# Normed residuals handed on by halves of the tokens, 1/rms taken under further projections, and linear attention values written twice with zero rows

## The chip, the cores and the metric

The kernel runs on one core of a Trainium2 chip. The metric is the device time of one execution in microseconds (us). The engines of the core are TensorE (PE, with its weight loads listed as PEld), VectorE (DVE), ScalarE (ACT), GpSimd (POOL) and SyncE (SP), which here issues the DMAs.

## The reference, cut to what matters

Two transformer blocks in sequence on one sequence of 512 tokens with 1024 features, all in fp32. The first is a hybrid layer whose mixer and feed-forward outputs are normed before they are added; the second has an even and an odd layer, with plain residuals.

```python
# first block (hybrid_layer)
mix = jnp.concatenate([o_a, o_s], axis=-1) @ w_out
x = x + rms_norm(mix, post_mix_norm)
h = rms_norm(x, pre_ffn_norm)
u = causal_dwconv(h @ w_up, ffn_conv_w, ffn_conv_b)
gate, up = jnp.split(u, 2, axis=-1)
f = (jax.nn.silu(gate) * up) @ w_down
x = x + rms_norm(f, post_ffn_norm)
# second block, for layer 0 (even) and 1 (odd)
x = x + mixer(rms_norm_2(x, mix_norm))
x = x + conv_ffn(rms_norm_2(x, ffn_norm[layer]), ...)
# odd mixer: gated linear attention over 8 chunks of 64 tokens, 4 heads, dk 128, dv 256
def step(state, inp):
    q_c, k_c, v_c, decay_c = inp
    state = decay_c[..., None] * state + jnp.einsum('bchk,bchv->bhkv', k_c, v_c)
    return state, jnp.einsum('bchk,bhkv->bchv', q_c, state)
```

## The kernel before, in words

The residual X is kept as 8 tiles of 128 features (partitions) x 512 tokens. The program is a sequence of stages: mix1, ffn1 (the first block), even, ffn2, odd, ffn3 (the second). Every stage projects with weights that come by DMA. A projection is done in split precision: the weight is cast into a hi part by ACT (`wload`, L197) and its rest, the lo part, by DVE (L200), the activations likewise, and `mm3` (L209 to L211) issues three matmuls for each block of 128 features: hi x hi, hi x lo, lo x hi, each 128 x 128 weights against 512 tokens. Of a 1024 x 128 weight tile, the 8 blocks make 24 matmuls, here called one projection.

A norm before a projection isn't applied to the activations: the projection takes X times the gain, and the result is scaled by 1/rms of each token afterwards. So a stage's first projections need only the hi and lo parts of X times the gain (`prep_block`: hi by ACT L261, lo by DVE L262, the square by ACT L287, the sum of squares in `acc` by POOL or, for the last, DVE L289). `first` (L297) runs the first four projections of the next stage block by block as these come; inside, `stat_r` (L323) takes column sums of `acc` by PE (st, L328) and makes 1/rms, and `bcast` (L334) spreads it over the partitions by a ones matmul (bc, L341).

mix1 and ffn1 end in `post_norm`: the output projection's blocks m = 0 to 7 are the generator `gen`; each block is squared (ACT L430) and summed (POOL L435); after block 7 two ones matmuls for each half of the tokens (pb, L441 and L443) give the sum over features; ACT makes 1/rms (L445 to L447), DVE corrects it (L449, L450), and then for each of the 8 blocks DVE forms F times gain times r (L457; L451 for block 0) and adds it to X (L458; L452), and `emit` prepares the next stage's activations. The first of these can start only when all of block 7 is done.

In the odd mixer, each head has 8 chunks of 64 tokens. The values V are written from PSUM by ACT (L1128), two blocks of 128 tokens in one tile. For each chunk the matmul pS (L1218) contracts the 64 tokens, that is 64 partitions, of the decayed keys KD and of V, DVE updates the state S (L1224), and two matmuls po (L1227) apply it to the chunk's queries. While this chain runs, the projection of the next head's values (or, for the last head, the output projection) is put between.

The order on each engine is made by a scheduler that goes through the program with priorities, each instruction going where its inputs and buffers allow; the chain of the odd mixer is put at a higher priority (HP). PSUM tiles for projections come from the pools pp and pm; weight tiles have 4 buffers for hi and 4 for lo, raw weights 2, activations 32 ("act").

Of the kernel before, what the change touches and what calls it, by code (L numbers as in the profile page):

```python
# [90 lines left out]
class Prog:  # L91
# [98 lines left out]
    def wload(s, src, f):  # L190
# [4 lines left out]
        hi = s.sb.tile([P, 1024], F32R, tag="wh", bufs=NBUF["wh"], name=s.nm("wh"))  # L195
        lo = s.sb.tile([P, 1024], F32R, tag="wl", bufs=NBUF["wl"], name=s.nm("wl"))
# [31 lines left out]
    def proj_part(s, src, per, n, acts):  # L228

        for i in range(KB // per):  # L230
            hi, lo = s.wload(src[i], per * n * P)
            for j in range(per):
# [4 lines left out]
                yield i * per + j, out  # L237

# [53 lines left out]

    def take(s):

        return s.acts, s.R, s.rb

    def first(s, srcs, late=True):  # L297
# [23 lines left out]
        s.ready += outs  # L321

# [42 lines left out]
    def ffn(s, wu, wd, cw, cb, norm=False):  # L365
# [40 lines left out]
    def add_res(s, X, gen, nxt):  # L406
        for m, ps in gen:
            if m == 0:
                s.begin(nxt)
            s.nc.vector.tensor_add(X[m], X[m], ps)  # L410
            s.emit(m, X[m])
        s.finish(False)

    def post_norm(s, gen, gain, X, nxt, part=None):
# [4 lines left out]
        F = []  # L419
        ng = s.small(KB, tag="ng", bufs=1)  # L420
        v.tensor_scalar(ng, s.pv[:, PVO[gain]:PVO[gain] + KB], -1.0, None, ALU.mult)
        for m, ps in gen:
            sq = s.t(tag="u") if m else acc
            if part is None:
                f, fs = s.act(F32), ps
            else:
                f = fs = part[m]
                v.tensor_add(f, f, ps)
            for h in ([slice(0, S // 2), slice(S // 2, S)] if m == KB - 1 else [slice(0, S)]):
                sc.activation(sq[:, h], fs[:, h], AF.Square)  # L430
            if part is None:
                sc.copy(f, ps)
            F.append(f)
            if 0 < m < KB - 1:
                nc.gpsimd.tensor_tensor(acc, acc, sq, ALU.add)  # L435

        pbs = [s.pt("pb"), s.pt("pb")]
        r = s.sb.tile([P, S], F32, tag="rb", bufs=2, name=s.nm("rb"))
        halves = [slice(0, S // 2), slice(S // 2, S)]
        for pb, h in zip(pbs, halves):  # L440
# [974 lines left out]
```

## Time and profile before

| What | Value |
|---|---|
| median of 3 runs (lowest to highest) | 2184.18 us (2183.92 to 2188.77) |
| the profiled execution: its time, its span | 2189.66 us, 2187.9 us |
| granted clock, mean over the span | 0.98 |
| PE busy | 2106.9 us, 96% |
| DVE, ACT, POOL busy | 65%, 43%, 9% |

The span is from the first to the last instruction of the profiled execution; times in rows are microseconds from the span's start. PE's matmuls are pipelined, so a row's duration is longer than the distance from one start to the next; costs are read from starts. The granted clock is a share of full speed: 1.00 is 2.4 GHz and 0.50 is 1.2 GHz.

### The profile page before, as it was taken

To read this page: it belongs to the slowest core of one execution; us is meant where nothing else is said; L and a number is where in the kernel's file an instruction comes from. 1 tells how busy PE (TensorE), PEld (TensorE's weight loads), DVE (VectorE), ACT (ScalarE), POOL (GpSimd) and SP (SyncE) were. 2 spreads that over 40 slices of the span, in tenths; PEclk is the share of its full clock that TensorE was granted. 3 is DMA by queue.
4 is the path that set the end of the run, shared out by engine and by line. 5 is a ranking of instruction groups with operands and counts; after the bars stand their busy time and mean duration, and the time that the engine had idled before them with its cause. 6 is when DMAs were issued, how large, how long until landed. Compare 5 with 4: busy or idle time off the path is not lost.

```text
span 2187.9 us, 26672 instructions
## 1 busy us (share of the span) xinstructions
PE 2106.9 (96%) x10260; PEld 1734.5 (79%) x10260; DVE 1418.1 (65%) x2540; ACT 933.2 (43%) x1506; POOL 198.2 (9%) x137
## 2 busy tenths in 40 slices
PE   7999899989989999998999999999999999999999
PEld 6777788777768888886877788888889877888887
DVE  6788867787568777226887787763343566877621
ACT  5444453355435444224665444442242324444411
POOL 3211111133030000012000100000000001000000
PEclk9999999999989999999999999999999999999999
DMA  4222212132213222321211132223322112322332
GB/s 151 97 64 84 78 64 74 68 104 99 87 39 126 97 96 93 94 93 48 96 46 61 58 124 97 97 91 98 93 71 95 55 61 68 118 99 99 93 114 66
DMA packets 57526, 189.14 MB, mean 86 GB/s; under 512 B 7757, under 2 KB 8013, under 8 KB 57398
## 3 DMA queue, kind: packets, MB, share of 16 engines
q1 hardware_dynamic: 55042, 180.75, 25.1%
q0 software_dynamic: 2032, 6.59, 0.9%
q8 instruction: 81, 1.33, 0.2%
q14 instruction: 47, 0.39, 0.1%
q10 hardware_dynamic: 324, 0.09, 0.0%
HBM read 184.99 MB, written 2.41 MB: 86 GB/s over the span
## 4 chain that ended last, share of the span: by engine, by line
PE 82%; DVE 13%; ACT 2%; DMA 1%; issue 1%; POOL 0%; SPq 0%; DVEq 0%; ACTq 0%; POOLq 0%
PE pp L209 24%; PE pp L211 23%; PE pp L210 23%; DVE wl L200 1%; DVE a L262 1%; DVE xbc L361 1%; DVE qkv L361 1%; DVE s L654 1%; PE pS L1218 1%; PE pz L979 1%; PE po L1227 1%; PE py L854 1%; DVE s L655 1%; PE pU L680 1%; DMA a<-bdd 1%
## 5 line engine op out<-in xcount | busy, mean ns | idle before, releaser
L209 PE MATMUL pp<-a,wh 128*128 128x512 f32 x2048 | 817.3, 400 | 15.6 <-ACT a L261 10.5
L210 PE MATMUL pp<-a,wh 128*128 128x512 f32 x2048 | 812.0, 397 | 1.3 <-DVE a L270 0.9
L211 PE MATMUL pp<-a,wl 128*128 128x512 f32 x2048 | 811.9, 397 | 0.9 <-DVE wl L200 0.9
L197 ACT CAST wh<-wr 128x1024 fp32r<-128x1024 f32 (+2 forms) x331 | 340.0, 1028 | 552.6 <-PE pp L210 420.6
L200 DVE TENSOR_TENSOR wl<-wr,wh 128x1024 fp32r<-128x1024 f32 (+3 forms) x300 | 362.2, 1207 | 230.4 <-ACT wh L197 223.0
L209 PEld LDWEIGHTS pp<-a,wh 128*128 128x128 f32 x2048 | 389.5, 190 | 102.7 <-ACT a L261 11.3
L210 PEld LDWEIGHTS pp<-a,wh 128*128 128x128 f32 x2048 | 389.3, 190 | 84.6 <-issue 3.9
L211 PEld LDWEIGHTS pp<-a,wl 128*128 128x128 f32 x2048 | 389.2, 190 | 81.8 <-DVE wl L200 1.7
L348 DVE TENSOR_TENSOR u<-pp,rb 128x512 f32<-128x512 f32 x200 | 137.1, 686 | 178.0 <-PE pp L211 177.5
L361 DVE SCALAR_TENSOR_TENSOR c<-u,pv,c 128x511 f32<-128x511 f32 (+1 forms) x264 | 196.4, 747 | 4.0
L211 PE MATMUL pp<-t,wl 128*128 128x512 f32 x336 | 132.5, 394 | 0.0
L209 PE MATMUL pp<-t,wh 128*128 128x512 f32 x336 | 132.4, 394 | 0.0
L210 PE MATMUL pp<-t,wh 128*128 128x512 f32 x336 | 131.3, 391 | 0.0
L289 POOL TENSOR_TENSOR t<-t,t 128x512 f32<-128x512 f32 x30 | 52.0, 1735 | 784.3 <-ACT t L287 783.3
L209 PE MATMUL pp<-wh,a 128*128 128x256 f32 (+2 forms) x384 | 114.8, 301 | 6.3 <-ACT wh L197 6.3
L211 PE MATMUL pp<-wh,a 128*128 128x256 f32 (+2 forms) x384 | 114.8, 300 | 3.3 <-DVE a L262 3.3
L210 PE MATMUL pp<-wl,a 128*128 128x256 f32 (+2 forms) x384 | 113.9, 297 | 1.3 <-DVE wl L200 1.3
L358 ACT ACTIVATE c<-u,pv 128x512 f32<-128x512 f32 x132 | 107.5, 814 | 8.8 <-DVE u L348 7.9
L200 POOL TENSOR_TENSOR wl<-wr,wh 128x1024 fp32r<-128x1024 f32 x31 | 76.8, 2476 | 306.7 <-ACT wh L197 270.3
L381 ACT ACTIVATE c<-c 128x512 f32<-128x512 f32 x66 | 41.7, 632 | 108.8 <-DVE c L361 108.8
L209 PEld LDWEIGHTS pp<-wh,a 128*128 128x128 f32 x384 | 76.3, 200 | 9.8 <-ACT wh L197 7.0
L211 PEld LDWEIGHTS pp<-wh,a 128*128 128x128 f32 x384 | 76.5, 199 | 5.5 <-DVE a L262 3.5
(316 smaller groups left out, 2316.8 us busy)
## 6 DMA issues: line engine op xcount, KB each, us to landing
wr<-in_w_up SPq DMA_DIRECT2D x132, 512.0 KB, 3.2
wr<-in_w_dn SPq DMA_DIRECT2D x48, 448.0 KB, 3.3
wr<-in_w_qkvz SPq DMA_DIRECT2D x32, 512.0 KB, 3.5
wr<-in_w_dn SPq DMA_DIRECT2D x24, 512.0 KB, 3.4
t<-gcd POOLq DMA_DIRECT2D x24, 256.0 KB, 4.2
wr<-in_w_xbc SPq DMA_DIRECT2D x12, 512.0 KB, 3.1
a<-bdd SPq DMA_DIRECT2D x16, 256.0 KB
wr<-in_w_o1a SPq DMA_DIRECT2D x8, 512.0 KB, 5.9
```

Of the source, the lines that this page charges most:

```text
L197: nc.scalar.copy(hi[:, :f], raw[:, :f])
L200: e.tensor_tensor(lo[:, :f], raw[:, :f], hi[:, :f], ALU.subtract)
L209: mm(out, l[0], r[0], start=first, stop=False)
L210: mm(out, l[0], r[1], start=False, stop=False)
L211: mm(out, l[1], r[0], start=False, stop=last)
L262: nc.vector.scalar_tensor_tensor(lo, src, scale, hi, ALU.mult, ALU.subtract)
L289: (nc.vector if s.pool_sq or last else nc.gpsimd).tensor_tensor(s.acc, s.acc, sq, ALU.add)
L348: s.nc.vector.tensor_tensor(u, ps, rb, ALU.mult)
L358: nc.scalar.activation(c, u, AF.Identity, scale=w(taps - 1), bias=bias)
L361: nc.vector.scalar_tensor_tensor(c[:, sh:], u[:, :S - sh], w(j), c[:, sh:], ALU.mult, ALU.add)
L381: nc.scalar.activation(g, g, AF.Silu)
L654: v.tensor_tensor(t3[:, :, k + 1:], A4[k // 8][:, k % 8, :, k + 1:], Y3[:, :, k:k + 1].to_broadcast([P, NT, 15 - k]), ALU.mult)
```

## The change

`post_norm` works by halves of the tokens (a: 0 to 255, b: 256 to 511). The blocks 2 to 7 of mix1's output projection (`proj_part_halves`) and block 7 of ffn1's are computed for half a first, then for half b; when half a is complete, its pb, 1/rms, F times r, the addition to X and the preparation of activations (`prep_half`) follow for that half. The next stage's first four weights are loaded at that point. `first_halves` takes the place of `first` after these two stages: four projections for half a (the fourth two blocks behind), then for half b, and then two more whole projections (for ffn1) or one more (for even), among which the row statistics and the broadcast stand. The squares of X are summed after all of X is there, on DVE. The POOL adds of these places move to DVE, but for some of ffn1's blocks. The third weight tile of ffn1's last block has its own buffer.

In the odd mixer, V is written twice for every block of 128 tokens, in a tile of 512 columns: columns 0 to 255 with 1/rms on the rows of the first chunk and zero on those of the second, columns 256 to 511 the other way round (`Rm`). One matmul of 128 rows and 512 columns then gives the products of both chunks.

```diff
-    def wload(s, src, f):
+    def wload(s, src, f, own=False):
...
+        if own:
+            hi, lo = (s.ph.tile([P, 1024], F32R, tag=n, bufs=1, name=s.nm(n)) for n in ("wxh", "wxl"))
...
+    def proj_part_halves(s, src, per, n, acts, whole):
...
+        for h in HALVES:
+            for i, w in ws:
+                for j in range(per):
+                    yield i * per + j, dot(w, j, h), h
...
+    def prep_half(s, k, x, h):
...
+        nc.scalar.activation(hi[:, h], x[:, h], AF.Copy, scale=g)
+        nc.vector.scalar_tensor_tensor(lo[:, h], x[:, h], g, hi[:, h], ALU.mult, ALU.subtract)
+
+    def sumsq(s, X):
+
+        for k, x in enumerate(X):
+            sq = s.t(tag="u") if k else s.acc
+            s.nc.scalar.activation(sq, x, AF.Square)
+            if k:
+                s.nc.vector.tensor_tensor(s.acc, s.acc, sq, ALU.add)
...
+    def first_halves(s, nxt):
...
+        for k in range(KB + 2):
+            for i in range(4):
+                j = k - 2 * (i == 3)
+                if 0 <= j < KB:
+                    mm(i, j, a)
+        for k in range(KB - 2):
+            for i in range(4):
+                mm(i, k, b)
+        for i in range(4):
+            for k in (KB - 2, KB - 1):
+                mm(i, k, b)
+        for j, ap in enumerate(nxt):
+            hi, lo = s.wload(ap, D)
...
+                if j == 0 and k == 2:
+                    s.R = s.stat_r(s.acc)
+                if (j, k) == ((1, 0) if len(nxt) > 1 else (0, 4)):
+                    s.rb = s.bcast(s.R)
...
             if 0 < m < KB - 1:
-                nc.gpsimd.tensor_tensor(acc, acc, sq, ALU.add)
...
+                (v if part or m == KB - 2 else nc.gpsimd).tensor_tensor(acc[:, h], acc[:, h], sq[:, h], ALU.add)
+            if m < KB - 1:
+                continue
+            if h is HALVES[0]:
+                s.begin(nxt)
+                for ap in nxt[1]:
+                    s.prefetch(ap)
...
+            for k in range(KB):
+                v.scalar_tensor_tensor(F[k][:, h], F[k][:, h], ng[:, k:k + 1], r[:, h], ALU.mult, ALU.mult)
+                v.tensor_add(X[k][:, h], X[k][:, h], F[k][:, h])
+                s.prep_half(k, X[k], h)
+        s.sumsq(X)
+        s.first_halves(nxt[2])
...
-                sc.activation(V[tb // 2][:, (tb % 2) * 256:(tb % 2) * 256 + 256], ps[:, :256], AF.Copy, scale=R[:, tb:tb + 1])
+                for half in range(2):
+                    sc.activation(V[tb][:, half * 256:half * 256 + 256], ps[:, :256], AF.Copy, scale=Rm[:, tb, half:half + 1])
...
-                    te.matmul(pS[:, :256], KD[tb][rows, h * P:(h + 1) * P], Vn[tb // 2][rows, (tb % 2) * 256:(tb % 2) * 256 + 256],
-                              start=True, stop=True)
+                    if half == 0:
+                        pS = s.pt("pS")
+                        te.matmul(pS, KD[tb][:, h * P:(h + 1) * P], Vn[tb], start=True, stop=True)
+                    kv = pS[:, half * 256:half * 256 + 256]
```

Where the scheduler puts the instructions is shown at three places. The first is PE at the end of ffn1. Before, it reads the last products of block 7 (pp_8368, against the weight tile wh_8364), the four pb matmuls, and the first products of the even mixer (a_8462 and a_8463 are the hi and lo parts of X's block 0):

```order
L210 MATMUL pp_8368<-t_7718,wh_8364 128x512
L211 MATMUL pp_8368<-t_7717,wl_8365 128x512
L441 MATMUL pb_8440<-t_6082,cst 128x256 [waits Pool_49]
L441 MATMUL pb_8441<-t_6082,cst 128x256 [waits PE_49]
L443 MATMUL pb_8440<-t_8435,cst 128x256 [waits Activation_49]
L443 MATMUL pb_8441<-t_8435,cst 128x256 [waits Activation_49]
L209 MATMUL pp_8554<-a_8462,wh_8532 128x512 [waits Activation_49]
L209 MATMUL pp_8555<-a_8462,wh_8538 128x512
L209 MATMUL pp_8556<-a_8462,wh_8544 128x512
L210 MATMUL pp_8554<-a_8463,wh_8532 128x512 [waits DVE_49]
L211 MATMUL pp_8554<-a_8462,wl_8533 128x512
```

Now the products are of 256 columns; after half a comes its first pb, and half b of block 7 (pp_8746) follows at once with the second pb among its products; after half b (below the dots) stands its pb, and then half a of the even mixer's projections (pp_8877 to pp_8880):

```order
L214 MATMUL pp_8594<-t_7943,wxl_8591 128x256
L535 MATMUL pb_8690<-t_6369,cst 128x256 [waits DVE_49,PE_49]
L212 MATMUL pp_8746<-a_6387,wh_8578 128x256
L536 MATMUL pb_8690<-t_8662,cst 128x256 [waits Activation_49]
L213 MATMUL pp_8746<-a_6388,wh_8578 128x256
L214 MATMUL pp_8746<-a_6387,wl_8579 128x256
...
L214 MATMUL pp_8746<-t_7943,wxl_8591 128x256
L535 MATMUL pb_8815<-t_6369,cst 128x256
L212 MATMUL pp_8877<-a_8700,wh_8668 128x256 [waits Activation_49]
L536 MATMUL pb_8815<-t_8662,cst 128x256 [waits Activation_49]
L213 MATMUL pp_8877<-a_8701,wh_8668 128x256 [waits DVE_49]
```

What PE waits for between block 7 and the next stage's products has moved under half b.

The second is DVE at the end of mix1. Before, after the last block's addition (L428) and a weight's lo part (L200), it reads the correction of 1/rms and then the 512-column operations on F (a_4955 is block 0, a_4988 block 1), X and the activations:

```order
L428 TENSOR_TENSOR a_5186<-a_5186,pp_5821 128x512 [waits DVE_49,PE_49]
L200 TENSOR_TENSOR wl_5949<-wr_5946,wh_5948 128x1024 [waits DMAHW6_49,DVE_49,Activation_49]
L449 SCALAR_TENSOR_TENSOR t_5677<-pb_5838,epsd,t_5677 128x256 [waits Activation_49]
L449 SCALAR_TENSOR_TENSOR t_5677<-pb_5839,epsd,t_5677 128x256 [waits Activation_49]
L450 SCALAR_TENSOR_TENSOR rb_5840<-t_5677,rb_5840 128x256 [waits DVE_49] x2
L451 SCALAR_TENSOR_TENSOR a_4955<-a_4955,s_5678,rb_5840 128x256 [waits DVE_49] x2
L452 TENSOR_TENSOR x_5666<-x_5666,a_4955 128x256 [waits DVE_49] x2
L457 SCALAR_TENSOR_TENSOR a_4988<-a_4988,s_5678,rb_5840 128x512
L457 SCALAR_TENSOR_TENSOR a_5021<-a_5021,s_5678,rb_5840 128x512
L262 SCALAR_TENSOR_TENSOR a_5861<-x_5666,pv,a_5860 128x512 [waits Activation_49]
L458 TENSOR_TENSOR x_5666<-x_5666,a_4988 128x512 [waits DVE_49]
```

Now, by halves, half a's operations (L543, L544 and L325, the new lines of F times r, of the addition to X, and of the lo part) stand among half b's additions of the projection (L515) and two of the three weight subtractions (L203):

```order
L515 TENSOR_TENSOR a_5054<-a_5054,pp_5936 128x256 [waits PE_49]
L543 SCALAR_TENSOR_TENSOR a_4955<-a_4955,s_5679,rb_5678 128x256 [waits DVE_49]
L543 SCALAR_TENSOR_TENSOR a_4988<-a_4988,s_5679,rb_5678 128x256
L203 TENSOR_TENSOR wl_5848<-wr_5845,wh_5847 128x1024 [waits DMAHW4_49,Activation_49]
L515 TENSOR_TENSOR a_5087<-a_5087,pp_5953 128x256 [waits PE_49]
L544 TENSOR_TENSOR x_5666<-x_5666,a_4955 128x256 [waits DVE_49]
L515 TENSOR_TENSOR a_5120<-a_5120,pp_5970 128x256 [waits PE_49]
L544 TENSOR_TENSOR x_5666<-x_5666,a_4988 128x256 [waits DMAHW5_49,DVE_49]
L203 TENSOR_TENSOR wl_5854<-wr_5851,wh_5853 128x1024 [waits DMAHW5_49,Activation_49]
L515 TENSOR_TENSOR a_5153<-a_5153,pp_5987 128x256 [waits PE_49]
L325 SCALAR_TENSOR_TENSOR a_5874<-x_5666,pv,a_5873 128x256 [waits Activation_49]
L515 TENSOR_TENSOR a_5186<-a_5186,pp_6004 128x256 [waits PE_49]
```

The work that half a's first products wait for now shares DVE's queue with that of half b and of the weights.

The third is PE in the odd mixer. Before, each chunk has its own pS of 256 columns before its two po (S_14114 and so on are the states):

```order
L209 MATMUL pp_14026<-wh_13990,a_12422 128x256
L1227 MATMUL po_14104<-u_13179,S_14114 128x64 [waits DVE_49]
L1227 MATMUL po_14105<-u_13179,S_14114 128x64
L1218 MATMUL pS_14124<-t_13787,t_13068 128x256
L210 MATMUL pp_14026<-wl_13991,a_12422 128x256
...
L211 MATMUL pp_14026<-wh_13996,a_12609 128x256
L1227 MATMUL po_14104<-u_13179,S_14120 128x64 [waits DVE_49]
L1227 MATMUL po_14105<-u_13179,S_14120 128x64
L1218 MATMUL pS_14130<-t_13788,t_13069 128x256
L1227 MATMUL po_14104<-u_13179,S_14126 128x64 [waits DVE_49]
L1227 MATMUL po_14105<-u_13179,S_14126 128x64
```

Now one pS of 512 columns stands ahead of two chunks' po; the names L212 to L214 are the three projection matmuls, L1309 is pS and L1318 po:

```order
L212 MATMUL pp_14427<-wh_14423,a_13120 128x256
L1318 MATMUL po_14535<-u_13606,S_14539 128x64 [waits DVE_49]
L1318 MATMUL po_14536<-u_13606,S_14539 128x64 [waits PE_49]
L1309 MATMUL pS_14547<-a_14215,t_13495 128x512 [waits PE_49]
L1318 MATMUL po_14535<-u_13606,S_14543 128x64 [waits DVE_49]
L1318 MATMUL po_14536<-u_13606,S_14543 128x64
L213 MATMUL pp_14427<-wl_14424,a_13120 128x256
L214 MATMUL pp_14427<-wh_14423,a_13121 128x256
L1309 MATMUL pS_14557<-a_14216,t_13496 128x512 [waits PE_49,Activation_49]
L1318 MATMUL po_14535<-u_13606,S_14549 128x64 [waits DVE_49]
L1318 MATMUL po_14536<-u_13606,S_14549 128x64
```

Every second pS is gone, and the po of two chunks follow one pS.

## Rows read from the trace of the kernel before

**Rows 1.** The page: busy us of each engine (share of the span) and its instructions.
```profile
PE 2106.9 (96%) x10260; PEld 1734.5 (79%) x10260; DVE 1418.1 (65%) x2540; ACT 933.2 (43%) x1506; POOL 198.2 (9%) x137
```

**Rows 2.** Waits of PE around the end of mix1 (595 to 660).
```profile
PE pp L209 <- ACT a L261: 5.3, 1, 5.3
PE st L328 <- DVE t L289: 3.6, 1, 3.6
```

**Rows 3.** Waits of PE around the end of ffn1 (978 to 1045).
```profile
PE st L328 <- DVE t L289: 4.2, 1, 4.2
```

**Rows 4.** Windows, end of mix1: busy PE, PEld, DVE, ACT, POOL; clock; DMA.
```profile
619.00:624.00 5.00, 0.18 (x1) 0.18 (x2) 4.00 (x10) 2.23 (x7) 0.00 (x0) 0.82 0.30 105
624.00:629.00 5.00, 5.00 (x12) 3.82 (x13) 5.00 (x8) 3.50 (x7) 2.05 (x1) 0.50 0.00 0
```

**Rows 5.** Timeline of PE, end of mix1: start, us, what.
```profile
599.64 0.39 PE L209 MATMUL pp<-a,wh 128*128 128x512 f32 x1
...
615.74 0.39 PE L211 MATMUL pp<-a,wl 128*128 128x512 f32 x1
616.33 1.13 PE L441 MATMUL pb<-t,cst 128*128 128x256 f32 x4 [0.21 <-POOL t L435]
617.41 1.13 PE L443 MATMUL pb<-t,cst 128*128 128x256 f32 x4
...
656.55 0.39 PE L209 MATMUL pp<-a,wh 128*128 128x512 f32 x1
```

**Rows 6.** Timeline of PE in a token-major projection: 256 columns.
```profile
1038.56 0.28 PE L209 MATMUL pp<-wh,a 128*128 128x256 f32 x1
1038.67 0.28 PE L210 MATMUL pp<-wl,a 128*128 128x256 f32 x1
```

**Rows 7.** Timeline of PE, end of ffn1 and start of the even mixer.
```profile
981.18 0.40 PE L209 MATMUL pp<-a,wh 128*128 128x512 f32 x1
...
1004.22 1.65 PE L209 MATMUL pp<-a,wh 128*128 128x512 f32 x3 [5.27 <-ACT a L261]
...
1024.07 1.05 PE L328 MATMUL st<-cst,t 128*128 128x1 f32 x8 [4.19 <-DVE t L289]
...
1032.12 1.02 PE L341 MATMUL bc<-t,cst 128*128 128x512 f32 x2
...
1033.22 0.39 PE L210 MATMUL pp<-a,wh 128*128 128x512 f32 x1
...
1035.77 1.13 PE L938 MATMUL pn<-t,ceven 128*128 128x512 f32 x2
```

**Rows 8.** Timeline of DVE at the end of mix1.
```profile
617.01 1.23 DVE L200 TENSOR_TENSOR wl<-wr,wh 128x1024 fp32r<-128x1024 f32 x1 [0.17 <-ACT wh L197]
...
621.46 0.87 DVE L451 SCALAR_TENSOR_TENSOR a<-a,s,rb 128x256 f32<-128x256 f32 x2
...
624.25 0.74 DVE L262 SCALAR_TENSOR_TENSOR a<-x,pv,a 128x512 fp32r<-128x512 f32 x1
...
628.04 1.77 DVE L262 SCALAR_TENSOR_TENSOR a<-x,pv,a 128x512 fp32r<-128x512 f32 x1
```

**Rows 9.** Timeline of PE in the odd mixer: pS among projections, then the chain.
```profile
1698.18 0.39 PE L211 MATMUL pp<-a,wl 128*128 128x512 f32 x1
1698.49 0.70 PE L1218 MATMUL pS<-t,t 64*128 64x256 f32 x2
...
1699.34 0.28 PE L210 MATMUL pp<-wl,a 128*128 128x256 f32 x1
...
1728.91 0.69 PE L1218 MATMUL pS<-t,t 64*128 64x256 f32 x2
...
1730.12 0.70 PE L1218 MATMUL pS<-t,t 64*128 64x256 f32 x2
```

**Rows 10.** Groups of ACT by line and shape: count, busy us, mean ns.
```profile
L1128 ACT ACTIVATE t<-pp,R 128x256 f32<-128x256 f32 x16 | 7.3, 473 | 20.1 <-PE pp L211 20.1
```

**Rows 11.** Window in the odd mixer (columns as in Rows 4).
```profile
1755.00:1762.00 7.00, 7.00 (x29) 5.90 (x29) 1.65 (x3) 1.29 (x3) 0.00 (x0) 0.53 0.00 0
```

More of the change, by code (lines that the diff above doesn't have):

```diff
@@ L237, in proj_part, with dot @@
                 yield i * per + j, out
+    def proj_part_halves(s, src, per, n, acts, whole):
+        def dot(w, j, h):
+            out = s.ps()
+            for q in range(n):
+                c = slice((j * n + q) * P, (j * n + q + 1) * P)
+                s.mm3(out[:, h], [t[:, c] for t in w], [t[:, h] for t in acts[q]], q == 0, q == n - 1)
+            return out
+        ws = []
+        for i in range(KB // per):
+            w = s.wload(src[i], per * n * P)
+            if i < whole:
+                for j in range(per):
+                    yield i * per + j, dot(w, j, ALL), ALL
+            else:
+                ws.append((i, w))
+        for h in HALVES:
+            for i, w in ws:
+                for j in range(per):
+                    yield i * per + j, dot(w, j, h), h
     def proj_tm(s, srcs, acts, evac):
@@ L406, in add_res @@
     def add_res(s, X, gen, nxt):
-        for m, ps in gen:
+        for m, ps, *_ in gen:
             if m == 0:
@@ L418, in post_norm @@
         acc = s.t(tag="u")
-        F = []
+        F = part or [None] * KB
+        sqs = {}
+        r = s.sb.tile([P, S], F32, tag="rb", bufs=2, name=s.nm("rb"))
         ng = s.small(KB, tag="ng", bufs=1)
         v.tensor_scalar(ng, s.pv[:, PVO[gain]:PVO[gain] + KB], -1.0, None, ALU.mult)
-        for m, ps in gen:
-            sq = s.t(tag="u") if m else acc
+        for m, ps, h in gen:
             if part is None:
-                f, fs = s.act(F32), ps
-            else:
[L427 to L430, printed above, removed]
+                if F[m] is None:
+                    F[m] = s.act(F32)
+                fs = ps
+            else:
+                fs = F[m]
+                with s.tc.high_priority(offset=HB):
+                    v.tensor_add(fs[:, h], fs[:, h], ps[:, h])
+            if m == KB - 1:
+                if m not in sqs:
+                    sqs[m] = s.t(tag="u")
+                sq = sqs[m]
+            else:
+                sq = s.t(tag="u") if m else acc
+            sc.activation(sq[:, h], fs[:, h], AF.Square)
             if part is None:
-                sc.copy(f, ps)
-            F.append(f)
+                sc.copy(F[m][:, h], ps[:, h])
             if 0 < m < KB - 1:
-                nc.gpsimd.tensor_tensor(acc, acc, sq, ALU.add)
[L437 to L440, printed above, removed]
+                (v if part or m == KB - 2 else nc.gpsimd).tensor_tensor(acc[:, h], acc[:, h], sq[:, h], ALU.add)
[5 more added lines that the diff above has]
+                    s.prefetch(ap)
+            pb = s.pt("pb")
             nc.tensor.matmul(pb[:, h], s.c("ones"), acc[:, h], start=True, stop=False)
-        for pb, h in zip(pbs, halves):
             nc.tensor.matmul(pb[:, h], s.c("ones"), sq[:, h], start=False, stop=True)
-        for pb, h in zip(pbs, halves):
             sc.activation(r[:, h], pb[:, h], AF.Ln, bias=s.epsc, scale=1.0 / D)
@@ L907, in mix1 @@
         s.log_exp()
-        s.post_norm(s.proj_part(a["w_o1c"], 2, 4, pc), "post_mix", X, after, part=F)
+        s.post_norm(s.proj_part_halves(a["w_o1c"], 2, 4, pc, 1), "post_mix", X, after, part=F)
         return X
```

68 lines of the change are left out of this document (43 added, 25 removed).

## The prediction

> **What bounds the kernel now.** I read the page first: TensorE (PE) is busy 96% of the span, and no other engine comes near [rows 1]. So time can only come from fewer or cheaper PE instructions, from PE's idle time, or from stretches at a lowered clock. The waits of PE around the two calls of `post_norm` come next: at the end of mix1 PE stands 5.3 us until the first hi part of the new activations is there, and later 3.6 us until the sum of squares is there [rows 2]; at the end of ffn1 the same two waits are 5.3 and 4.2 us [rows 3, 7]. The windows show what follows such a wait: PE was busy 0.18 of 5 us, and in the next 5 us the granted clock is 0.50, that is 1.2 GHz instead of 2.4 GHz [rows 4]. So each of the two stage ends costs about 9 us of idle time and some us of half speed. In the odd mixer PE has no such waits; there the cost of its instructions counts.
>
> **The ends of mix1 and ffn1: prices.** A 512-column projection matmul comes 0.227 us after the one before it (599.64 to 615.74 is 71 of them) [rows 5]. The new one has 256 columns. That shape stands in the trace, in the token-major projections: 0.12 us from start to start [rows 6]. Two halves cost 0.24 us, 0.013 more than a whole. Split are 72 matmuls in mix1 (blocks 2 to 7), 66 in ffn1 (block 7) and twice 96 of the next stage's first four projections: 330 x 0.013 = 4.3 us of new PE work, contained in the sums below. The two ones matmuls of a half (pb, 128x256, four instructions) take 1.08 us (616.33 to 617.41) [rows 5].
>
> **End of mix1.** Before, from the start of block 2 (599.64) to the start of what follows the first four projections (656.55) is 56.9 us [rows 5]. To compare I add the two further projections that the changed kernel computes before anything else: 48 x 0.227 = 10.9, together 67.8 us. After, in PE's new order: half a of six blocks, 72 x 0.12 = 8.6; its pb 1.1 and some 0.5 of waiting for DVE's last add; half b 8.6; half a of the four projections, 96 x 0.12 = 11.5; pb of half b 1.1; half b of the four 11.5; then 10.9 with the row statistics among them (st, 1.05 us at 1024.07) and the broadcast (bc: 1032.12 to 1033.22, less one spacing, 0.87 us) [rows 7]. That is 55.8 us without further waits.
>
> The waits come from DVE. For each block k it does three operations of half width (F times r, X plus F, the lo part); two of that width take 0.87 us in a row [rows 8], so three take at most 1.3, and about 1.1 where they are plain adds. PE needs 9 x 0.12 = 1.08 us for three projections of block k. DVE is thus no faster than PE, and it also has three weight subtractions of 1.23 us [rows 8] and half b's six adds in its queue before or among them. The chain from pb to the first hi part, which makes the 5.3 us wait now, starts under half b (8.6 us) and ends under it. Laying DVE's and ACT's instructions end to end in the new order with these durations, I get 2.3 us of PE waits in half a's projections, 0.9 at the start of half b's, because pb of half b stands behind half a's projections in PE's order, and 0.4 before the products with new weights: 3.6. The sum of squares is hidden by half b's projections and the first products after them; without that cover it would cost what its wait costs now, 3.6 us. Sum 59.4; saved are **8.4 us**.
>
> DVE operations of 0.74 us take 1.77 us while a POOL add runs [rows 8]; 12 of the adds go from POOL to DVE here and 7 at the end of ffn1. The sum uses the short durations with these adds in DVE's queue.
>
> **End of ffn1.** Before, block 7 starts at 981.18 and the first four projections end at 1035.77 [rows 7]: 54.6 us, and with the one further projection (24 x 0.227 = 5.4) 60.0. After: 66 x 0.12 = 7.9, pb 1.1, 7.9, 1.1, 11.5, 11.5, 5.4, st 1.05, bc 0.87, together 48.4; I add 1.5 for small waits (the first activation, and a PSUM bank for what follows). Here DVE is free of weight work and half b's pb comes right after half b, so its activations are made under 11.5 us of PE work. Saved: **10.1 us**. Bounds for both ends together: 24 us if no wait at all were left, and 9 us if PE fell to half clock for 5 us twice in each.
>
> **The odd mixer.** 32 matmuls of 64 rows x 256 columns become 16 of 128 x 512. Among projection matmuls one of the old kind costs 0.81 us: its neighbours start at 1698.18 and 1699.34 (1.16), less one spacing each of 0.227 and 0.12 [rows 9]. In the bare chain a chunk takes 1.21 us (1728.91 to 1730.12), of which pS is half or a little more, 0.62 to 0.73 [rows 9]. The new matmul isn't in the trace in this place; the nearest row is bc, fp32, 128 rows, 512 columns: 0.87 us [rows 7]. A pair of chunks then saves 0.75 us among projections, 0.37 to 0.59 in the chain. Of the 32, 8 stand among projections, 13 in the chain, 11 between the two: with 0.75, 0.5 and 0.6 a pair, 3.0 + 3.2 + 3.3 = **9.5 us**. The bounds are 0 (a pair costs no less than now) and 12 (0.75 each). The 16 further evacuations on ACT, 0.47 us each [rows 10], lie on an engine that is busy 43% of the span [rows 1], and the tiles are needed a head later; if that cover went, the most is 7.5 us. One stretch of 7 us here has a granted clock of 0.53 [rows 11], where PE could do 3.3 us more at full clock; it may go or come again, and I put nothing down for it.
>
> A rule speaks against this part. The Trainium skill, TensorEngine Tiling (Array Packing), Key Properties, says that row tiles operate independently and load and multiply in parallel, so two 64-row products side by side should cost about one; merging them would give nothing, and the time would be 9.5 us higher. The rows disagree: such a product costs 0.81 us each time. The same section says that a change of the tiling mode drains TensorE, which would fit the 0.81.
>
> **Sum.** 8.4 + 10.1 + 9.5 = 28.0 us. The profiled execution took 2189.66 us, 5.5 above the median of 2184.18; the stretches compared are differences within it, so I take 28.0 off the median: 2156.2. A measurement of this kernel can tell about 0.3%, 6.6 us, from no change.
>
> **Rivals.**
> (A) As summed, 2149 to 2162. Chance 0.57.
> (B) The waits go but the clock doesn't come back: PE, paced by DVE, has small gaps all through half a, and 5 to 10 us at each end run at half speed, as after each long wait now [rows 4]. That costs 2.5 to 5 us each, 2161 to 2166. For it: DVE is no faster than PE there. Against: the longest single gap in the sum is 1.2 us, not 5. Chance 0.15.
> (C) The odd part gives 0 to 3 us, because the zero rows cost what the second matmul did, or the chain of S updates on DVE sets the pace: 2162 to 2165. For it: 13 of 32 stand in the bare chain. Against: PE is never idle there. Chance 0.12.
> (D) More is gained: the half-speed stretch of the odd mixer goes as well, and the waits left at the two ends are under 1 us: 2143 to 2149. Chance 0.08.
> (E) Slower: a 256-column matmul with its own weight load doesn't come every 0.12 us, since its load must hide behind a product half as long. At a spacing of s, 330 pairs cost 330 x (2s - 0.227); the gain (28.0 + 4.3) is eaten at s = 0.162. At 0.19 the 330 pairs cost 50 us, and the time would be 2184.2 - 32.3 + 50.5 = 2202. Against it: in [rows 6] every product has a new weight. Chance 0.04.
> (F) The change doesn't do its work: half a's r comes so late on DVE that half b's projections end first, and a wait of 5 us with its half-speed stretch stands between the halves at both ends: 7 to 10 us each, 2170 to 2176. Chance 0.04.
> A page speaks for E: the Trainium skill, TensorE: Matmul & The Clock Gate, Back-to-back issue gap, says that load and product together set the spacing, with 81 ns for 128 and 131 ns for 512 columns; an estimate between them for 256 columns is 98 ns, so 330 splits would cost 21 us and the time would be 2173. The rows here have 120 and 227 ns, and by them the price is 4.3.
>
> **Range and chances.** The likeliest is A. 2145 to 2167 takes in A, nearly all of B and C and half of D: some 0.86. Faster by over 0.3% (below 2177.6): A, B, C, D, F and none of E, 0.94 after something taken off for what isn't listed; within 0.3%: 0.03; slower: 0.03.
>
> **What would show it.** The four PE waits of 3.6 to 5.3 us are gone; the granted clock is 1.0 through both stage ends; no DVE operation of 1.77 us is left there; split projections start every 0.12 us; pS has 32 instructions, a matmul costing about 0.87; ACT's V evacuations are 32. Wrong would be a spacing above 0.15 us (E), gaps over 2 us in half a or a clock of 0.5 (B, F), and a pS of 1.5 us (C).

## The result, and the profile after

The changed kernel took 2154.33 us in the median of 4 runs (2151.0 to 2157.06); the kernel before, on the same chip, 2186.22. The ratio is 0.9852, with an interval of 0.9834 to 0.9871: faster by 1.5%. The prediction was 2156.2 us, 28.0 below the median then known; measured were 31.9. Beside the experiments below the kernel before was run again and took 2188.3 us (e1 to e4), 2188.4 (e5 to e9) and 2188.6 (e10, e11), so they are compared by their ratios and by pieces of the span.

The first row of the page, of the changed kernel, answers to [rows 1]: PE is busy 20 us less, and POOL 34 us less.

```profile
PE 2087.3 (97%) x10558; PEld 1733.9 (80%) x10558; DVE 1418.9 (66%) x2615; ACT 944.4 (44%) x1544; POOL 164.5 (8%) x118
```

PE's waits at the end of mix1 (597 to 660) answer to [rows 2]; the 5.3 and 3.6 us are gone, and in their place stand three short ones:

```profile
PE pp L212 <- ACT a L324: 2.2, 2, 1.1
PE po L214 <- DVE wl L203: 0.4, 1, 0.4
```

Windows of the same place (PE, PEld, DVE, ACT, POOL busy; granted clock; DMA) answer to [rows 4]: PE is busy throughout, and the clock stays at 1.00 in every window from 597 to 656, where before it was 0.50 (1.2 GHz) in the 5 us behind the first wait.

```profile
606.00:616.00 10.00, 9.90 (x79) 9.73 (x79) 7.60 (x17) 5.90 (x12) 0.00 (x0) 1.00 0.16 52
616.00:619.00 3.00, 2.12 (x17) 1.91 (x16) 2.97 (x7) 1.67 (x3) 0.00 (x0) 1.00 0.51 175
619.00:631.00 12.00, 11.35 (x82) 10.43 (x82) 9.20 (x26) 4.38 (x10) 0.00 (x0) 1.00 0.13 46
631.00:644.00 13.00, 12.34 (x98) 11.86 (x98) 12.72 (x29) 9.95 (x18) 0.00 (x0) 1.00 0.00 1
```

The timeline of PE there shows the new order: block 2's first half product, the ones matmuls of half a, the wait in half a of the next stage (619.26 is its third block), the ones matmuls of half b, the first product of half b (631.65), the first whole product behind the four projections (643.36), st and bc.

```profile
597.17 0.28 PE L212 MATMUL pp<-a,wh 128*128 128x256 f32 x1
597.28 0.28 PE L213 MATMUL pp<-a,wh 128*128 128x256 f32 x1
...
606.10 0.67 PE L535 MATMUL pb<-t,cst 128*128 128x256 f32 x2
...
619.26 0.62 PE L212 MATMUL pp<-a,wh 128*128 128x256 f32 x3 [1.14 <-ACT a L324]
...
626.34 0.64 PE L535 MATMUL pb<-t,cst 128*128 128x256 f32 x2
...
631.65 0.74 PE L212 MATMUL pp<-a,wh 128*128 128x256 f32 x4 [1.01 <-ACT a L324]
...
643.36 0.40 PE L212 MATMUL po<-a,wh 128*128 128x512 f32 x1
...
646.11 0.95 PE L403 MATMUL st<-cst,t 128*128 128x1 f32 x8
...
651.13 1.02 PE L416 MATMUL bc<-t,cst 128*128 128x512 f32 x2
```

From 597.17 to 643.36 are 46.2 us; the prediction's terms for the same way (all but 48 x 0.227, st, bc and the last 0.4) add up to 46.1. At the end of ffn1, the timeline of PE answers to [rows 7]:

```profile
970.52 0.28 PE L212 MATMUL pp<-a,wh 128*128 128x256 f32 x1
...
978.41 0.59 PE L535 MATMUL pb<-t,cst 128*128 128x256 f32 x2
...
987.43 0.59 PE L535 MATMUL pb<-t,cst 128*128 128x256 f32 x2
...
1011.51 0.40 PE L212 MATMUL po<-a,wh 128*128 128x512 f32 x1
...
1017.71 1.12 PE L416 MATMUL bc<-t,cst 128*128 128x512 f32 x2
...
1020.76 0.39 PE L212 MATMUL pp<-wh,a 128*128 128x256 f32 x1 [1.45 <-DVE u L423]
```

From block 7 (970.52) to the end of the four half projections (1011.51) are 41.0 us without a wait. Then come the further projection, st and bc, and one wait of 1.45 us, until DVE has emptied a PSUM bank.

In the odd mixer, the timeline of PE answers to [rows 9]. Among projections a pS now costs 0.85 us (1698.49 to 1699.58, less two spacings of 0.12), and in the chain 0.91 (1701.38 to 1702.29):

```profile
1698.49 0.28 PE L212 MATMUL pp<-wh,a 128*128 128x256 f32 x1
1698.61 1.02 PE L1309 MATMUL pS<-a,t 128*128 128x512 f32 x2
...
1699.58 0.28 PE L214 MATMUL pp<-wh,a 128*128 128x256 f32 x1
...
1701.38 1.08 PE L1309 MATMUL pS<-a,t 128*128 128x512 f32 x2
1702.29 0.55 PE L1318 MATMUL po<-u,S 128*128 128x64 f32 x4
```

ACT writes V 32 times (groups of ACT, as [rows 10]), and it delayed nothing on PE, which is busy for the whole stage:

```profile
L1219 ACT ACTIVATE a<-pp,s 128x256 f32<-128x256 f32 x32 | 13.4, 473 | 17.4 <-PE pp L214 17.4
```

The windows of the chain's stretch have no half clock left, against 0.53 in [rows 11]:

```profile
1700.00:1720.00 20.00, 20.00 (x146) 17.82 (x146) 13.37 (x22) 9.02 (x18) 0.00 (x0) 1.00 0.22 57
1720.00:1740.00 20.00, 20.00 (x138) 17.53 (x137) 13.24 (x21) 9.05 (x17) 0.00 (x0) 1.00 0.19 66
1740.00:1760.00 20.00, 20.00 (x99) 15.87 (x98) 15.15 (x26) 5.54 (x9) 0.00 (x0) 1.00 0.27 87
```

**Where the time came from.** Every kernel here has the same unedited work between the edited places, so I cut the span at starts of the same instruction, and the pieces can be compared between kernels: from the first product of mix1's block 2 to that of ffn1's block 7 (before 599.64 to 981.18, [rows 5, 7]); from there to ffn2's st (before at 1227.26, after at 1207.28); and the odd mixer from its own bc to ffn3's bc (before 1591.00 to 1836.15, after 1571.05 to 1802.49).

| kernel | ratio (95% interval) | end of mix1 + ffn1 | end of ffn1 + even | odd mixer |
|---|---|---|---|---|
| before | 1 | 381.5 | 246.1 | 245.2 |
| changed | 0.9852 (0.9834 to 0.9871) | 373.3 | 236.8 | 231.4 |
| e5: changed, again | 0.9870 (0.9849 to 0.9892) | 373.2 | 237.0 | 231.5 |
| e1: halves only | 0.9917 (0.9902 to 0.9932) | 373.3 | 237.0 | 248.0 |
| e2: V only | 0.9929 (0.9912 to 0.9946) | 381.6 | 246.1 | 228.3 |
| e3: 32 pS of 128 rows | 0.9872 (0.9857 to 0.9888) | 373.3 | 236.5 | 232.1 |
| e4: end of mix1 as before | 0.9891 (0.9873 to 0.9908) | 381.5 | 236.4 | 229.9 |
| e6: sums on POOL | 0.9881 (0.9852 to 0.9909) | 375.9 | 237.1 | 229.8 |
| e7: two blocks halved | 0.9855 (0.9831 to 0.9879) | 373.0 | 236.5 | 229.8 |
| e9: no further projections | 0.9943 (0.9922 to 0.9964) | 382.6 | 246.9 | 229.8 |
| e10: sums first | 0.9836 (0.9812 to 0.9859) | 370.9 | 236.5 | 228.3 |
| e11: sums first, four blocks | 0.9855 (0.9829 to 0.9882) | 373.2 | 236.2 | 229.8 |

The three pieces gave 8.2, 9.3 and 13.7 us (from starts that aren't rounded), 31.2 together. The spans of the two profiles differ by 33.7; the other 2.5 lie in mix1 ahead of the first edit (599.64 against 597.17), where both kernels do the same. ffn2 took 358.6 to 359.0 us and ffn3, from its bc to the end of PE's last product, 347.3 to 347.4 in all twelve profiles.

### The profile page after: what moved, and what is told of

Read it like the earlier page. It is cut to its first block, busy times and chain, and to the rows that moved or that the text cites. A ratio compares the mean times of both kernels' runs of the same rounds, so it can differ in the third digit from the quotient of the medians.

```text
span 2154.2 us, 27349 instructions
## 1 busy us (share of the span) xinstructions
PE 2087.3 (97%) x10558; PEld 1733.9 (80%) x10558; DVE 1418.9 (66%) x2615; ACT 944.4 (44%) x1544; POOL 164.5 (8%) x118
## 4 chain that ended last, share of the span: by engine, by line
PE 82%; DVE 12%; DMA 2%; ACT 2%; issue 1%; POOL 0%; SPq 0%; DVEq 0%; ACTq 0%; POOLq 0%
PE pp L212 24%; PE pp L214 24%; PE pp L213 24%; DVE wl L203 1%; DVE qkv L436 1%; DVE xbc L436 1%; DMA a<-bdd 1%; DVE s L741 1%; PE pz L1066 1%; PE py L941 1%; PE pU L767 1%; DVE s L742 1%; PE pS L1309 1%; PE pT L762 1%; PE po L1318 1%
## 5 line engine op out<-in xcount | busy, mean ns | idle before, releaser
L212 PE MATMUL pp<-a,wh 128*128 128x512 f32 (+1 forms) x2128 | 824.4, 389 | 6.3 <-ACT a L324 2.2
L213 PE MATMUL pp<-a,wh 128*128 128x512 f32 (+1 forms) x2128 | 820.2, 386 | 1.3 <-DVE a L294 0.9
L214 PE MATMUL pp<-a,wl 128*128 128x512 f32 (+1 forms) x2128 | 819.1, 385 | 0.7 <-DVE wl L203 0.7
L200 ACT CAST wh<-wr 128x1024 fp32r<-128x1024 f32 (+3 forms) x330 | 339.1, 1029 | 535.3 <-PE pp L213 404.9
L203 DVE TENSOR_TENSOR wl<-wr,wh 128x1024 fp32r<-128x1024 f32 (+4 forms) x299 | 359.8, 1204 | 217.2 <-ACT wh L200 213.8
L212 PEld LDWEIGHTS pp<-a,wh 128*128 128x128 f32 x2128 | 402.8, 190 | 88.5 <-issue 5.8
L213 PEld LDWEIGHTS pp<-a,wh 128*128 128x128 f32 x2128 | 403.2, 189 | 79.9 <-issue 3.9
L214 PEld LDWEIGHTS pp<-a,wl 128*128 128x128 f32 x2128 | 403.1, 189 | 76.7 <-issue 1.2
L214 PE MATMUL pp<-t,wl 128*128 128x512 f32 (+1 forms) x336 | 130.9, 389 | 0.0
L212 PE MATMUL pp<-t,wh 128*128 128x512 f32 (+1 forms) x336 | 130.7, 389 | 0.0
L213 PE MATMUL pp<-t,wh 128*128 128x512 f32 (+1 forms) x336 | 129.7, 386 | 0.0
L212 PE MATMUL pp<-wh,a 128*128 128x256 f32 (+2 forms) x384 | 113.1, 296 | 7.9 <-ACT wh L200 6.5
L214 PE MATMUL pp<-wh,a 128*128 128x256 f32 (+2 forms) x384 | 112.9, 294 | 4.4 <-DVE a L286 4.4
L203 POOL TENSOR_TENSOR wl<-wr,wh 128x1024 fp32r<-128x1024 f32 x31 | 76.8, 2477 | 304.4 <-ACT wh L200 268.0
L313 POOL TENSOR_TENSOR t<-t,t 128x512 f32<-128x512 f32 x18 | 29.4, 1634 | 728.0 <-ACT t L311 727.6
L212 PEld LDWEIGHTS pp<-wh,a 128*128 128x128 f32 x384 | 74.4, 195 | 10.0 <-ACT wh L200 6.5
L214 PEld LDWEIGHTS pp<-wh,a 128*128 128x128 f32 x384 | 74.7, 194 | 6.2 <-DVE a L286 4.6
```

Source lines behind the costliest of these rows:

```text
L200: nc.scalar.copy(hi[:, :f], raw[:, :f])
L203: e.tensor_tensor(lo[:, :f], raw[:, :f], hi[:, :f], ALU.subtract)
L212: mm(out, l[0], r[0], start=first, stop=False)
L213: mm(out, l[0], r[1], start=False, stop=False)
L214: mm(out, l[1], r[0], start=False, stop=last)
L313: (nc.vector if s.pool_sq or last else nc.gpsimd).tensor_tensor(s.acc, s.acc, sq, ALU.add)
```

## The experiments

**Which edit gave what (e1, e2, e4).** The edits of e1 and e2 are the two halves of the diff; e4 keeps `post_norm` and `first` of before for mix1's end:

```diff
-        s.post_norm(s.proj_part_halves(a["w_o1c"], 2, 4, pc, 1), "post_mix", X, after, part=F)
+        s.post_norm_whole(s.proj_part(a["w_o1c"], 2, 4, pc), "post_mix", X, after, part=F)
```

> The halves at the ends of mix1 and ffn1 as in the changed kernel, the odd mixer as before. Theory (three separate savings, which the trace of the changed kernel puts at 8.2 us at the end of mix1, 9.3 at the end of ffn1 and 13.7 in the odd mixer): 17.5 us below the kernel before, about 2168.5. Rival (part of what the traces show in the odd mixer is really owed to the halves, for instance by a different state of the clock): the odd mixer's stretch from the broadcast at its start to the one of ffn3 is shorter than the 245.2 us of before without the edit there, and the time is nearer to 2160.

> The values written twice and one pS of 128 rows for two chunks; both stage ends as before. Theory: the odd mixer alone gives its 13.7 us, 2172.5, with pS and po both cheaper from start to start (in the changed kernel's trace pS 11.4 us in all instead of 19.3, po 12.5 instead of 16.5) and no stretch at half clock in the chain. By the prediction's own price of 9.5 us it would be 2176.7. Rival (the odd mixer gains only together with the halves): 2184 or more.

> The changed kernel with the end of mix1 as before (whole tokens, first four projections, statistics in them), the end of ffn1 by halves and the odd mixer as changed. Theory: 8.2 us above the changed kernel, 2162.5, with the waits of 5.3 and 3.6 us and the two half-clock stretches back at the end of mix1 alone. Rival (the gain at the end of mix1 is given back later in ffn1, whose start finds its weights late): within 3 us of the changed kernel.

Measured medians: e1 2171.2, e2 2173.0, e4 2164.3 us. The pieces of the table repeat: halves alone shorten the first two pieces, V alone the third only, and e4's first piece is that of before to 0.1 us. In e2 pS and po take as long as in the changed kernel, counted from start to start: 11.0 and 12.3 us (e2's expectation puts 11.4 and 12.5 there), and the clock of its chain is at 1.00. The waits of PE in e4 at the end of mix1 are those of [rows 2] again:

```profile
PE pp L212 <- ACT a L285: 5.3, 1, 5.3
PE st L403 <- DVE t L313: 3.6, 1, 3.6
```

So the three savings are separate and add up; nothing is given back later in ffn1. The first rival of e1 falls: the odd mixer didn't get shorter by the halves, but 2.8 us longer. The windows of e1 there show why it varies at all: two stretches at a lowered clock, where the kernel before had one.

```profile
1710.00:1720.00 10.00, 10.00 (x47) 7.65 (x47) 2.93 (x7) 0.10 (x1) 0.00 (x0) 0.76 0.28 91
...
1740.00:1750.00 10.00, 10.00 (x48) 8.62 (x47) 2.83 (x5) 2.18 (x4) 0.00 (x0) 0.66 0.01 2
```

If I add up (1 - clock) x 10 us over windows of 10 us across the odd mixer, 8.5 us were lost before, 12.0 in e1, 5.1 in the changed kernel, 1.7 in e2 and 3.5 in e4. Without these, the stage takes 236.7 and 236.0 us with the old pS, and 226.3, 226.6 and 226.4 with the new one. So the edit is worth 10 us at full clock, and 3.4 us of the 13.7 are half-speed time.

**What the old pS cost (e3).**

```diff
-                    if half == 0:
-                        pS = s.pt("pS")
-                        te.matmul(pS, KD[tb][:, h * P:(h + 1) * P], Vn[tb], start=True, stop=True)
-                    kv = pS[:, half * 256:half * 256 + 256]
+                    cols = slice(half * 256, half * 256 + 256)
+                    pS = s.pt("pS")
+                    te.matmul(pS[:, cols], KD[tb][:, h * P:(h + 1) * P], Vn[tb][:, cols], start=True, stop=True)
+                    kv = pS[:, cols]
```

> The changed kernel, but each chunk has its own pS of 128 rows and 256 columns (32 matmuls, half of whose rows meet zeros), so no matmul of 64 rows is left and the number of matmuls is as before. Theory (what the old pS cost is the change between 64-row and 128-row matmuls, paid by pS and by its neighbours): as fast as the changed kernel within 2 us, since 32 products of 256 columns stream as many columns as 16 of 512. Rival (each pS has a price of its own, whatever its rows): 8 to 12 us above the changed kernel, 2162 to 2166.

The odd mixer took 232.1 us, 0.7 above the changed kernel, and 227.0 without its half-speed time: the number of matmuls is not what counted. The whole time, 2161.2 us, is not within 2 us of the first measurement of the changed kernel, but its ratio of 0.9872 is that of the second (0.9870); in its profile, mix1 ahead of the edits took 603.1 us. The timeline of e3's chain (po, pS, po, pS) has a chunk in 0.87 us instead of the 1.21 of [rows 9], with the same number of matmuls and twice the rows:

```profile
1688.83 0.66 PE L1318 MATMUL po<-u,S 128*128 128x64 f32 x4
1689.33 0.65 PE L1309 MATMUL pS<-a,t 128*128 128x256 f32 x2
1689.81 0.55 PE L1318 MATMUL po<-u,S 128*128 128x64 f32 x4
1690.20 0.65 PE L1309 MATMUL pS<-a,t 128*128 128x256 f32 x2
```

Counted from start to start over the whole stage, pS took 19.3 us before, 11.0 in the changed kernel and 11.4 in e3; po, which no edit touches, took 16.5, 12.3 and 12.8. Without the time lost at half clock before's are 18.7 and 15.3 us. So a 64-row matmul also made its 128-row neighbours dearer. In one place of before two pS stand next to each other (four instructions):

```profile
1723.85 0.70 PE L1218 MATMUL pS<-t,t 64*128 64x256 f32 x4
1724.48 0.38 PE L211 MATMUL pp<-wh,a 128*128 128x256 f32 x1
```

Both together take 0.63 us, as much as one alone in the chain (0.62). Two readings fit this row: the change between the forms has a price that a pair pays once, or the two, on different halves of the rows, run side by side. That po gets dearer beside pS speaks for a price of the change; no run here takes the two apart.

**What hides the way to the first activations (e7, e10, e11).** e7 halves only blocks 6 and 7 in mix1; e10 gives the squares and sums the priority of the additions; e11 does the latter with four blocks halved.

```diff
-        s.post_norm(s.proj_part_halves(a["w_o1c"], 2, 4, pc, 1), ...)
+        s.post_norm(s.proj_part_halves(a["w_o1c"], 2, 4, pc, 3), ...)
```
```diff
-            sc.activation(sq[:, h], fs[:, h], AF.Square)
+            with s.tc.high_priority(offset=HB if part else 0):
+                sc.activation(sq[:, h], fs[:, h], AF.Square)
...
-                (v if part or m == KB - 2 else nc.gpsimd).tensor_tensor(acc[:, h], acc[:, h], sq[:, h], ALU.add)
+                with s.tc.high_priority(offset=HB if part else 0):
+                    (v if part or m == KB - 2 else nc.gpsimd).tensor_tensor(acc[:, h], acc[:, h], sq[:, h], ALU.add)
```

> The changed kernel, but in mix1 only the last two blocks of the output projection are computed by halves instead of six, so that half b of them lasts 2.9 us instead of 8.6. Theory (the way from the ones matmuls to the first new activations is hidden by half b alone): PE stands for 2 to 4 us before the next stage's first product, and the end of mix1 is 2 to 4 us longer, less 0.6 for 48 products not split. Rival (DVE's queue sets the pace in the half projections anyway, whatever lies ahead): within 1 us.

> The changed kernel with the squares and sums of the output projection at mix1's end put at the same high priority as the additions before them, so that half b's ones matmuls stand right behind half b's projections and not behind half a's of the next stage. Theory (the 1.0 us wait at half b's first projection comes from these late ones matmuls): that wait is gone, and the waits ahead of half a's projections stay or grow by what the sums take of DVE's queue (six adds of about 0.4); the end of mix1 is 0.5 to 1.5 us shorter than 373.4 us with ffn1. Rival (DVE has the same work in all and sets the pace, so a wait taken away here comes back there): within 0.5 us.

> As the run before, and only four of mix1's blocks by halves (half b lasts 5.8 us). With two blocks halved PE waited 2.5 us and then ran 3 us at half clock, and the end was still 1.3 us shorter than with six. Theory (what was gained there is the early half b and fewer split products; a half b of 5.8 us covers the way to the first activations): no wait above 1 us, no half clock, and mix1's end with ffn1 takes 370 to 371.5 us, 2 to 3 us below the changed kernel; the whole time is 2 to 3 us below it, which the timed runs can hardly tell. Rival (DVE's queue, not the cover, delays half a's activations): 372.5 to 373.5 us as with six blocks.

In e7 PE waits as the theory said, 2.5 us, and the clock falls after it; here the waits and the windows:

```profile
PE pp L212 <- ACT a L324: 1.9, 1, 1.9
PE pb L536 <- ACT t L522: 0.6, 1, 0.6
```

```profile
616.00:623.00 7.00, 4.42 (x25) 3.30 (x24) 4.94 (x12) 4.88 (x12) 0.00 (x0) 1.00 0.23 80
623.00:627.00 4.00, 4.00 (x21) 3.94 (x22) 4.00 (x12) 1.42 (x4) 0.00 (x0) 0.59 0.22 89
```

But the end of mix1 is 0.3 us shorter than in the changed kernel, not 2 to 4 longer: block 2 starts 48 whole products ahead of the first half product (612.00), at 601.12, and 373.0 us later comes ffn1's block 7. (The 1.3 us that e11's expectation names, and builds on, don't come out of these starts.) The theory of the cover is right about the wait and wrong about the sum; the number is the rival's. From its first half product of the next stage (622.91) to the first whole one (647.65) e7 takes 24.7 us, which is 192 x 0.12 and the half speed: no wait is left in there. The changed kernel takes 27.7 (615.66 to 643.36), with half b's ones matmuls and 3.6 us of waits among them. So the waits moved ahead and, with the half speed behind them (1.6 us lost in the second window), came to about as much, and 48 products fewer are split (0.6 us). e10 takes away waits themselves: half b's ones matmuls stand two products behind half b's projections, not behind half a's of the next stage, the wait of 1.0 us at half b's first product is gone, one wait of 1.0 remains, and the end of mix1 is 2.5 us shorter, more than expected.

```profile
PE pp L212 <- ACT a L324: 1.0, 1, 1.0
```

In e11 both together bring 373.2 us, no better than the changed kernel; PE waits 1.4 us at half a's first products and 1.1 for the sums, the clock falls behind these waits, and DVE is busy for all of the 3 us in which they lie (third number of the first window):

```profile
PE pp L212 <- ACT a L324: 1.4, 1, 1.4
PE pb L537 <- DVE t L528: 1.1, 2, 0.9
```

```profile
618.00:621.00 3.00, 1.46 (x5) 0.68 (x5) 3.00 (x7) 2.07 (x6) 0.00 (x0) 1.00 0.62 190
621.00:625.00 4.00, 4.00 (x21) 4.00 (x22) 4.00 (x11) 2.09 (x5) 0.00 (x0) 0.57 0.34 120
```

So its theory falls, and the number is the rival's. But its words "not the cover" aren't shown: e11 differs from e10 in the number of halved blocks alone and is 2.4 us longer. With a half b of 5.8 us PE waits 2.5 us and loses another 1.7 at the lowered clock; with one of 8.6 us a wait of 1.0 is left and the clock stays at 1.00. So the cover counts. That DVE, busy all the while, makes the way longer than 5.8 us is likely; which of its instructions do, no run takes apart. e10 is the best version found: 2152.5 us in the median and the lowest ratio, though its interval overlaps the changed kernel's; that its end of mix1 is shorter rests on the pieces.

**What the further projections and DVE's adds are worth (e9, e6).** e9 leaves the further projections out of the hand-over and puts st and bc behind the four; e6 puts the sums back on POOL.

```diff
-[up[l][0], up[l][FB], up[l][1], up[l][FB + 1]], [up[l][2], up[l][FB + 2]]
+[up[l][0], up[l][FB], up[l][1], up[l][FB + 1]], []
```
```diff
-                (v if part or m == KB - 2 else nc.gpsimd).tensor_tensor(acc[:, h], acc[:, h], sq[:, h], ALU.add)
+                nc.gpsimd.tensor_tensor(acc[:, h], acc[:, h], sq[:, h], ALU.add)
...
-                s.nc.vector.tensor_tensor(s.acc, s.acc, sq, ALU.add)
+                (s.nc.vector if k == KB - 1 else s.nc.gpsimd).tensor_tensor(s.acc, s.acc, sq, ALU.add)
```

> The changed kernel without the further projections in the two hand-overs: the row statistics and the broadcast stand right behind the four projections. Theory (the further projections hide the sum of squares, the statistics' small DVE operations and the broadcast): PE waits 1 to 3 us for the sum of squares, some 4 us for 1/rms, and 1 to 2 us for the first result to be taken out of PSUM, and part of what follows runs at half clock: 8 to 10 us more at each end, 2170 to 2174. Rival (the next projections start anyway, so only the order of work changes): within 3 us of the changed kernel.

> The changed kernel with the sums of squares of both stage ends back on POOL (all adds of the output projections' squares, and the first six of the seven adds of the residual's squares). Theory (a DVE operation beside a running POOL add takes 1.77 instead of 0.74 us, as in the rows of before): the two stage ends together are 3 to 6 us longer, with PE waits for DVE in the half projections, and some DVE operations of half width at twice their time. Rival (DVE's queue is what PE waits for, and POOL takes work off it): the ends are 0 to 2 us shorter.

e9 took 2175.5 us, a ratio of 0.9943; its two ends are 9.3 and 10.1 us longer, so more than all that the halves gave is lost again. PE's waits at the end of mix1 are the three of the theory, and the clock is at half from 655 to 665, over the last of these waits and the products behind them:

```profile
PE bc L419 <- DVE t L415: 3.2, 1, 3.2
PE pp L212 <- DVE u L426: 2.0, 1, 2.0
...
PE st L406 <- DVE t L333: 1.5, 1, 1.5
```

```profile
655.00:660.00 5.00, 2.07 (x2) 0.50 (x2) 3.79 (x9) 2.67 (x3) 0.00 (x0) 0.50 0.49 149
660.00:665.00 5.00, 3.95 (x9) 3.14 (x10) 4.97 (x10) 2.36 (x3) 0.00 (x0) 0.50 0.47 165
```

In e6, the end of mix1 is 2.6 us longer and that of ffn1 0.3: the theory's 3 to 6 us are nearly reached, but by another way. PE waits for the POOL sum itself ahead of the ones matmuls, and for one addition in DVE's queue:

```profile
PE pb L535 <- POOL t L526: 1.5, 2, 1.0
PE pp L212 <- DVE a L515: 1.2, 1, 1.2
```

With 0.2 us for weights these waits come to 2.9 us, against 2.6 in the changed kernel. What is longer comes behind them: the clock falls, as it doesn't in the changed kernel, and over the 7 us from 620 it costs 3.4 us:

```profile
620.00:627.00 7.00, 6.24 (x25) 5.88 (x26) 5.68 (x15) 2.95 (x7) 0.71 (x1) 0.51 0.31 104
```

DVE operations beside a POOL add are slow here too (half a width at 1.51 us instead of 0.48), but the slowest come after 632 us, where PE stands for less than 0.1 us at a time until 646. The rows are of DVE and of POOL, whose adds run from 632.48 to 635.26:

```profile
634.03 1.51 DVE L325 SCALAR_TENSOR_TENSOR a<-x,pv,a 128x256 fp32r<-128x256 f32 x1
```

```profile
632.48 2.78 POOL L333 TENSOR_TENSOR t<-t,t 128x512 f32<-128x512 f32 x2 [11.78 <-ACT t L331]
```

**The same kernel again (e5).**

> The changed kernel once more, unaltered. In the profiles so far the stretch ahead of the first edited place (mix1 up to block 2 of its output projection, the same instructions in the same order in every kernel) took 596.8 to 603.1 us, while the unedited stages after it (ffn1 between its ends, ffn2, ffn3) agree within 0.4 us. Theory (this spread belongs to the execution, not to a kernel): the stretch differs from the 597.2 us of the first profile by up to some us here too, and the edited stages repeat within 0.3 us, but for the odd mixer with its stretches at half clock. Rival (the change itself shortens the stretch by 2.4 us): 597 us again, within 0.5.

2158.1 us, a ratio of 0.9870. The edited pieces repeat within 0.2 us (373.2, 237.0, 231.5), and mix1 ahead of them took 599.1 us, not 597.2: that stretch belongs to the execution.

## Why the prediction was right

**The whole.** That 2154.3 us lies 1.9 from the 2156.2 is in part luck: the saving was 3.9 us larger than 28.0, and the median of before 2.0 higher than the one it was taken from. Of the terms, the two ends gave 0.2 and 0.8 us less than their sums and the odd mixer 4.2 more.

**The price of a split.** Right: half products start every 0.12 us (46.2 and 41.0 us above are made of it). The rival E, and the page's figures that spoke for it, are out: they would have added 17 us or more.

**End of mix1, 8.4 us.** Measured 8.2. The waits are of the kind summed: 1.1 and many gaps of 0.1 to 0.2 in half a, 1.0 at half b, 0.4 at the new weights. Counted from starts, as what goes beyond the spacing of products, they are 2.4, 1.4 and 0.6 us where I put 2.3, 0.9 and 0.4, while the two pairs of ones matmuls with the wait ahead of them took 2.1 instead of 2.7; so that 46.2 meets 46.1 is two small errors against each other. The cause given for the wait at half b, late ones matmuls, is what e10 shows by taking it away. The 2.5 us that e10 gains are not that wait alone: the 0.4 at the new weights is gone as well, and there are fewer gaps in half a.

**End of ffn1, 10.1 us.** Measured 9.3 with the even mixer. The 1.5 us for a PSUM bank are in the timeline, and from block 7 to the product behind that wait (1020.76) are 50.2 us where the sum has 49.9; the other 0.5 of the 0.8 us lies behind it in the even mixer, and I didn't follow it.

**The clock at both ends.** Rival B didn't come: waits of 1.1 us left the clock at 1.00, as the windows show, and at ffn1's end it is 1.00 in all windows from 970 to 1036. That it could come is seen in e6, e7, e9 and e11.

**The sum of squares.** Mis-sized: I priced its cover at 3.6 us. What the further projections hide is the whole way from the sum to the emptied PSUM bank, 9.3 and 10.1 us with the half clock behind the waits (e9).

**The odd mixer, 9.5 us.** Mechanism right, size off: measured 13.7. pS gave 8.3 of the 9.5 expected (19.3 to 11.0 us); what was missed is po, 4.2 us (16.5 to 12.3), for which no term was written: what stands beside a 64-row matmul is dearer too. Of these two sums 0.6 and 1.2 us are half-speed time of before's chain, for which I put nothing down; the rest of the 3.4 us lies on other products. Rival C falls with e2 and e3.

**The packing rule.** I said that the rows disagree with what the Trainium skill, TensorEngine Tiling (Array Packing), Key Properties, says of row tiles in parallel. That was half right. Two 64-row products side by side cost as one here (0.63 us for both), which agrees; but in only two places of the order did two of the 32 stand so, and a lone one cost 0.62 to 0.81. The other sentence there, that a change of the tiling mode drains TensorE, fits e3 and the cheaper po, but no run shows the drain itself. Keeping 64 rows and putting all pairs side by side, which the 0.63 us speak for, wasn't tried.

## What to carry to other kernels

Where an engine waits for a reduction over the last block of a projection, splitting the last blocks by tokens hides the way from the reduction to the next products, at 0.013 us for each product split; the statistics need further independent products behind them, or the wait only moves (e9). A matmul with fewer rows between full ones cost more than its own time here (64 rows, fp32), and zero rows were cheaper than the short contraction. When comparing kernels whose runs scatter by some us, cut the span at the same instructions: pieces repeat to some tenths of a us (the odd mixer once its half-speed time is taken off) where whole times scatter by 5 to 10.

## What was not expected of the hardware

Two neighbouring 64-row matmuls on the two row halves took 0.63 us together and one alone 0.62. A 128-row matmul beside a 64-row one was dearer (po 16.5 us in all, 15.3 without the half-speed time, against 12.3). A first stretch of 600 us, with the same instructions in the same order in all kernels, took 594.7 to 605.0 us over the twelve profiles, while 350 us of ffn2 and ffn3 repeated to 0.4; much of it is the clock: summed as above, 15.4 to 27.3 us are lost at half clock in that stretch, and without them it takes 575.8 to 580.3. Why the clock differs there wasn't looked into.
